# Where the small groups of experts stand in a streamed mixture of experts, and the order of its last products

## The chip, the cores and the metric

One core of a Trainium2 chip. The time is the device time of one execution in microseconds (us), as the median of several runs. TensorE (PE) multiplies, ScalarE (ACT) and VectorE (DVE) take results out of PSUM, GpSimd (POOL) does elementwise work in SBUF, and SyncE (SP) issues nearly all DMA transfers from HBM.

## The reference, cut to what matters

One decoder block for 256 tokens of width 1024, all in float32: attention and a gated recurrence, a normalisation, and then a mixture of 64 experts of which each token uses 8, beside a shared expert and an embedding term; a last normalisation ends it. The part that matters here:

```
idx, g = route(h, w_router[l], router_bias[l])            # 8 of 64 experts a token
for each expert e:                                        # xb: the tokens that chose e
    a = silu(xb @ w_gate[e]) * (xb @ w_up[e])             # 1024 -> 256
    out = (a @ w_down[e]) * g_b[:, None]                  # 256 -> 1024
    acc = acc.at[tok_b].add(out)
x = layer_norm(DEEPNORM_ALPHA * x1 + acc + shared + ple, ln2_w[l], ln2_b[l])
```

Each expert has 3 MB of weights, so 192 MB go through the core whatever the routing.

## The kernel before, in words

The first 380 us or so compute attention, the recurrence and the first normalisation. From then on the kernel streams expert weights. An expert's weights come as three transfers of 1 MB: n=0 and n=1 hold the gate and up columns of the first and the second half of the 1024 inputs, n=2 the down weights, whose columns 0 to 1023 give the first 512 outputs (f=0) and columns 1024 to 2047 the last 512 (f=1). Each transfer lands in one of 20 slots of 1 MB (`slot()`, rings of 9, 6, 2, 2 and 1), handed out in turn; a transfer into a slot waits until the products that read the slot's last content are done. SP issues all of them (`load`, line 81), each behind the one before; at most eight are under way.

The experts are sorted by how many tokens chose them (`rank`), all but the first eight. Those with most tokens are worked off two at a time, 64 token places each; the 24 with fewest are worked off four at a time, 32 places each (`SMALL` = 24). A unit (`units`) is two calls of `experts`: four experts where a call takes two, eight where a call takes four. There are ten units of pairs and three of groups of four. `SMALL_AT` gives the places at which the three are put among the others.

In a call of `experts`, `gate_up` (line 833) runs over the eight input blocks kt, and in each over the experts e, one product a step: the stationary operand is the expert's 64 or 32 token columns, the moving one 512 weight columns, and expert e writes its own 64 or 32 partitions of the PSUM tile `g`. Then `h` (line 800 and 802), two transposes of `h`, a copy `hT` (line 928), and the down products into a tile `g` for f=0 and one for f=1, over ft (the two halves of the 256 hidden values) and in each over the experts. Each `g` is scaled and split into `yh` (ACT, line 939) and `yl` (DVE, line 940), and four products with `sT` put it back to the tokens in `acc`; the two for f=1 are left to the next call (`rest`). In between, the calls gather the tokens of the next unit (tile `t` from `sel` and `xh`, `xl`). TensorE's order in this stage is that of the code (`PE_FIXED`).

In the last unit both calls load their weights as halves of 512 KB (`parts = 2`): of n=0 first half of every expert, then second half of every expert, and so on. Two slots more are taken there, for the rows of the last normalisation's weights and for their spread form `lw` (line 972); the first call spreads them by `norm_weights`, one row at each of its four steps. After the last call come `bn_stats`, `last_norm` and the stores.

Of the kernel before, what the change touches and what calls it, by code (L numbers as in the profile page):

```python
# [30 lines left out]
PE_FIXED = True  # L31
SB = 3
WARM, YB, TB, W2 = 8, 2, 2, 3
FIXED, SMALL, SMALL_AT = 8, 24, (2, 6, 9)
ROUTER_SPLIT = 4
WARM2 = 9
GS_POOL = (0, 2)
# [19 lines left out]
def tile_block(ctx: ExitStack, tc: tile.TileContext, a, out: bass.AP):  # L57
# [14 lines left out]
    def slot(dt=F32):  # L72

        pl, n = free[0]
        free.rotate(-1)
        return pl.tile([128, 2048], dt, name="raw", tag="raw", bufs=n)
# [3 lines left out]
    def load(dst, src, ordered=False):  # L80
        ins = nc.sync.dma_start(dst, src)
        loads.append(ins)
        if ordered:
            tc.keep_in_program_order(ins)
# [13 lines left out]
    def pinned(ins):  # L98
        if fixed["pe"]:
            tc.keep_in_program_order(ins)  # L100

    def mm(o, l, r, start=True, stop=True):
        pinned(pe.matmul(o, l, r, start=start, stop=stop))  # L103

    def transpose(o, t):
        pinned(pe.transpose(o, t, ident))  # L106
# [44 lines left out]
    for n in range(4):  # L151
        sl, c = slice(2 * n, 2 * n + 2), slice(512 * n, 512 * n + 512)
# [262 lines left out]
    def gates():  # L415
        gp = transposed(next_win())
        t = ptg.tile([128, 2, S], F32, name="tg", bufs=4)
        act.activation(t, gp, AF.Tanh, scale=0.5)
        return t
# [131 lines left out]
    def bank(tag, shape=(128, 512)):  # L551

        return pm2.tile(list(shape), F32, name=tag, tag=tag, bufs=2)
# [205 lines left out]
    def one_hot(pl, pos_of, n, by=pool, w=SLOTS):  # L759

        s = pl.tile([128, 2, w * n], F32R, name="sel1", bufs=2)
        for i in range(2):
            for e in range(n):
                by.tensor_scalar(s[:, i, w * e:w * e + w], iota[:, 0:w], pos_of(i)[:, e:e + 1], None, op0=OP.is_equal)  # L764
        return s
# [28 lines left out]
    def unit(u):  # L794
        r0, n = units[u]
        s, xe = one_hot(px2, lambda i: posm[:, i, r0:r0 + 2 * n], 2 * n, pool if u else dve, 128 // n), []
        return s, xe, gather(new_xe, bank, s, 4, xe)

    def swiglu(h, ps):
        act.activation(h, ps[:, 0:256], AF.Sigmoid)  # L800
        for n in range(2):
            dve.tensor_mul(h, h, ps[:, 256 * n:256 * n + 256])  # L802
# [18 lines left out]
    def expert_weights(r0, ne, last=False):  # L821

        w = [[] for _ in range(ne)]
        at = [expert_at(r0 + e) if r0 >= FIXED else None for e in range(ne)]
        for n in range(3):
            for e in range(ne):
                w[e].append(slot())
            parts = 2 if last else 1
            for part in range(parts):
                c = slice(2048 * part // parts, 2048 * (part + 1) // parts)  # L830
                for e in range(ne):
                    if at[e] is None:
                        load(w[e][n][:, c], a["exp"][3 * (r0 + e) + n][:, c])
                    else:
                        load(w[e][n][:, None, c], a["exp"][bass.ds(at[e] + n, 1)].rearrange("o p f -> p o f")[:, :, c], True)
        return w

    def gate_up(gu, kts, xe, off, w):
        n = 128 // len(w)
        for kt in kts:  # L840
            for e in range(len(w)):
                mm(gu[n * e:n * e + n], xe[kt // 2][:, kt % 2, off + n * e:off + n * e + n],
                   w[e][kt // 4][:, 512 * (kt % 4):512 * (kt % 4) + 512], start=kt == 0, stop=kt == KT - 1)
# [8 lines left out]
    s, xe, steps = unit(0)  # L852
# [17 lines left out]
    hT = bank("t", (128, 2, S))  # L870
# [7 lines left out]
    gu0 = bank("g")  # L878
# [16 lines left out]
    p3 = t2.enter_context(tc.tile_pool(name="p3", bufs=1, reuse_waits="tile"))  # L895


    def experts(pl, bk, xe, off, s, gates, w, add, before=(), steps=(iter(()),) * 4, begun=None):


        ne, sl = len(w), 128 // len(w)
        if begun is None:
            begun = bk("g")
            gate_up(begun, range(4), xe, off, w)
        next(steps[0], None)
        gu = begun
        gate_up(gu, range(4, KT), xe, off, w)
        h = pl.tile([128, 256], F32, name="h", bufs=1)
        swiglu(h, gu)
        next(steps[1], None)  # L910
        tr = bk("t", (128, 256 + 2 * ne))
        for i in range(2):
            transpose(tr[:, 128 * i:128 * i + 128], s[:, i, off:off + 128].bitcast(F32))
        for i in range(2):
            mm(tr[:, 256:256 + 2 * ne], s[:, i, off:off + 128], gates(i).rearrange("p e n -> p (e n)"), start=i == 0, stop=i == 1)
        sT = pl.tile([128, S], F32R, name="sT", bufs=TB)
        act.activation(sT, tr[:, 0:256], CP)
        gsl = pl.tile([128, 1], F32, name="gsl", bufs=3)
        for e in range(ne):
            dve.reduce_sum(gsl[sl * e:sl * e + sl], tr[sl * e:sl * e + sl, 256 + 2 * e:258 + 2 * e],  # L920
                           axis=mybir.AxisListType.X)
        for _ in before:
            pass
        tr = bk("t", (128, 2, 128))
        for ft in range(2):
            transpose(tr[:, ft], h[:, 128 * ft:128 * ft + 128])
        hT = pl.tile([128, 2, 128], F32, name="hT", bufs=1)
        dve.tensor_copy(hT, tr)
        next(steps[2], None)
        parts = []  # L930
        for f in range(2):
            y = bk("g")
            for ft in range(2):
                for e in range(ne):
                    mm(y[sl * e:sl * e + sl], hT[:, ft, sl * e:sl * e + sl],
                       w[e][2][:, 1024 * f + 512 * ft:1024 * f + 512 * ft + 512], start=ft == 0, stop=ft == 1)
            yh = pl.tile([128, 512], F32R, name="yh", bufs=YB)
            yl = pl.tile([128, 512], F32R, name="yl", bufs=YB)
            act.activation(yh, y, CP, scale=gsl)  # L939
            dve.scalar_tensor_tensor(yl, y, gsl, yh.bitcast(F32), op0=OP.mult, op1=OP.subtract)  # L940
            parts.append((yh, yl))

        def scatter(f):
            for i in range(2):
                add(i, f, sT[:, 128 * i:128 * i + 128], parts[f])
                yield

        next(steps[3], None)
        for _ in scatter(0):
            pass  # L950
        return scatter(1)

    stats = px.tile([128, 2, 2, 6], F32, name="stats")
    def norm_weights(rows, lw):

        for r in range(4):
            ps = bank("t")
            mm(ps, ident[:4, r:r + 1].to_broadcast([4, 128]), rows)
            act.activation(lw[:, r // 2, 512 * (r % 2):512 * (r % 2) + 512], ps, CP)
            yield  # L960
# [3 lines left out]
    for q, (r0, ne) in enumerate(units):  # L964
        if q + 1 < len(units):
            first = steps
            nxt, xnxt, steps = unit(q + 1)
            fill = ((none, steps, steps, none),) * 2
            if q == 0:
                fill = ((list(first) for _ in (0,)), steps, steps, none), fill[1]  # L970
        else:
            rows, lw = slot()[:4, :512], slot().rearrange("p (n d) -> p n d", n=2)
            for n, v in enumerate(("ln2w", "ln2b")):
                load(rows[2 * n:2 * n + 2], a[v].rearrange("(r f) -> r f", r=2), True)
            fill = (norm_weights(rows, lw),) * 4, (none,) * 4
        for pr in range(2):
            r = r0 + ne * pr
            last = q + 1 == len(units) and pr == 1
            w = expert_weights(r, ne, q + 1 == len(units)) if r else w0
            def add(i, f, l, halves, last=last):  # L980
                for n, r in enumerate(halves):
                    mm(acc[i][f], l, r, start=False, stop=last and n == 1)
                if last:
                    dve.bn_stats(stats[:, i, f], acc[i][f])

            rest = experts(p2, bank, xe, 128 * pr, s, lambda i: gates2[:, i, r:r + ne], w, add, rest, fill[pr],
                           None if r else gu0)
        s, xe = nxt, xnxt
    for _ in rest:
        pass  # L990
# [40 lines left out]
    with tc.If(nr > 1):  # L1031
# [7 lines left out]
        with tc.For_i(1, nr, 1):  # L1039
            dve.tensor_scalar(posm, posm, -float(SLOTS), None, op0=OP.add)  # L1040
            dve.memset(pair_no, 0.0)
            with tc.For_i(0, NE, 2) as c0:
                with tc.tile_pool(name="po", bufs=1) as po, \
# [4 lines left out]
                    w = []  # L1048
                    for e in range(2):
# [3 lines left out]
                        for n in range(3):  # L1053
                            t = slot()
# [16 lines left out]
                    s = one_hot(po, lambda i: pp[:, i], 2)  # L1071
                    xe = []
# [9 lines left out]
                    for _ in experts(po, obank, xe, 0, s, lambda i: gp2[:, i], w, add):  # L1082
                        pass
# [109 lines left out]
```

## Time and profile before

| | |
|---|---|
| median of 3 runs | 910.8 us (909.67 to 911.46) |
| the profiled execution's own time | 909.14 us |
| its span, first to last instruction | 907.4 us |
| mean granted TensorE clock | 0.985 of full |
| TensorE matmul busy | 856.1 us, 94% |
| expert transfers | 180 of 1 MB, 24 of 512 KB |

A busy TensorE is not one at its peak: products of different experts that run side by side count once in the busy time, however many they are. In the slices of the page (22.7 us each) the DMA engines are full from the twenty-first slice to the thirty-eighth; that is the stage of the experts. A float32 product appears in the trace as two MATMUL pieces, so `x32` in a row is 16 products. The chain of waits names for each stretch what was awaited last; the timeline gives single instructions.

### The profile page before, as it was taken

The page shows a single profiled execution, that of the slowest core. Times are in us where ns is not written, and L with a number is a line of the kernel's source. Part 1 is how long each engine was busy: PE and PEld are TensorE (multiplying, and loading weights), DVE is VectorE, ACT ScalarE, POOL GpSimd, SP SyncE. Part 2 cuts the span into 40 slices and gives each one's busy share as a digit, 9 for nine tenths or more (in the row PEclk, how much of TensorE's full clock was granted, in tenths as well). Part 3 has the DMA queues.
Part 4 walks back from the last instruction along what each step waited for, and adds up shares of the span by engine and source line. Part 5 has one row for each costly group of instructions (what it writes and reads, how often), then busy time and mean ns, then how long its engine had stood idle before and what let it go on. Part 6 is the DMA issues. An engine that isn't in the chain of part 4 may idle for free.

```text
span 907.4 us, 13967 instructions
## 1 busy us (share of the span) xinstructions
PE 856.1 (94%) x5200; PEld 567.4 (63%) x5200; DVE 380.8 (42%) x807; ACT 327.3 (36%) x652; POOL 171.9 (19%) x219
## 2 busy tenths in 40 slices
PE   9999999999999999799999999999689988799992
PEld 7899997878789999678545454544235433245431
DVE  5555555695966656887112222221112211112215
ACT  6444454567675555545212122121011211112221
POOL 0015463743400000542021011011010110101001
PEclk9999999999999999899999999999999998999997
DMA  8953433443334988344799999999999999999971
GB/s 335 420 221 122 140 103 130 149 140 129 128 129 163 388 299 303 117 182 186 297 391 407 415 421 421 420 421 420 420 421 420 420 421 421 421 420 421 410 300 48
DMA packets 42048, 270.84 MB, mean 298 GB/s; under 512 B 5061, under 2 KB 5189, under 8 KB 12281
## 3 DMA queue, kind: packets, MB, share of 16 engines
q1 hardware_dynamic: 41624, 269.20, 74.6%
q8 instruction: 42, 0.69, 0.3%
q10 hardware_dynamic: 288, 0.52, 0.2%
q14 instruction: 30, 0.24, 0.1%
q0 software_dynamic: 64, 0.20, 0.1%
HBM read 268.85 MB, written 1.05 MB: 297 GB/s over the span
## 4 chain that ended last, share of the span: by engine, by line
PE 76%; DMA 16%; DVE 5%; issue 1%; ACT 1%; SPq 0%; DVEq 0%
PE pj L103 26%; PE g L103 25%; DMA raw<-in_exp_dram 15%; PE t L103 6%; PE acc L103 6%; PE ah L103 4%; PE mix L472 2%; PE sc L103 2%; PE yp L103 1%; PE ap L381 1%; PE t L106 1%; PE pt L260 1%; DVE hr L365 1%; PE op L103 1%; DMA raw<-in_win_dram 0%
## 5 line engine op out<-in xcount | busy, mean ns | idle before, releaser
L103 PE MATMUL g<-raw,xe 128*64 128x512 f32 (+1 forms) x1024 | 203.9, 606 | 19.9 <-DMA raw<-in_exp_dram 19.9
L117 ACT ACTIVATE wh<-raw 128x512 fp32r<-128x512 f32 x213 | 132.3, 630 | 121.1 <-PE pj L103 86.5
L118 DVE TENSOR_TENSOR wl<-raw,wh 128x512 fp32r<-128x512 f32 x184 | 129.5, 715 | 90.7 <-ACT wh L117 69.8
L103 PEld LDWEIGHTS g<-raw,xe 128*64 128x64 f32 (+1 forms) x1024 | 59.7, 128 | 148.8 <-issue 109.0
L103 PE MATMUL pj<-xhi,wh 128*128 128x256 f32 x448 | 128.9, 288 | 0.2 <-DVE hq L366 0.2
L103 PE MATMUL pj<-xlo,wh 128*128 128x256 f32 x448 | 128.3, 286 | 0.0
L103 PE MATMUL pj<-xhi,wl 128*128 128x256 f32 x448 | 128.1, 286 | 0.0
L764 POOL TENSOR_SCALAR sel<-cst,posm 128x64 fp32r<-128x64 f32 (+1 forms) x120 | 48.0, 428 | 371.0 <-PE t L103 363.7
L802 DVE TENSOR_TENSOR h<-h,g 128x256 f32<-128x256 f32 x52 | 21.9, 421 | 228.6 <-ACT h L800 227.7
L103 PE MATMUL g<-raw,hT 128*64 128x512 f32 (+1 forms) x512 | 98.3, 598 | 4.3 <-DMA raw<-in_exp_dram 3.8
L800 ACT ACTIVATE h<-g 128x256 f32<-128x256 f32 x26 | 10.0, 383 | 222.5 <-PE g L103 222.5
L940 DVE SCALAR_TENSOR_TENSOR yl<-g,gsl,yh 128x512 fp32r<-128x512 f32 x52 | 39.0, 751 | 118.2 <-ACT yh L939 118.2
L103 PEld LDWEIGHTS pj<-xhi,wh 128*128 128x128 f32 x448 | 85.5, 191 | 3.5 <-issue 1.9
L103 PEld LDWEIGHTS pj<-xhi,wl 128*128 128x128 f32 x448 | 85.5, 191 | 3.1 <-issue 2.7
L103 PEld LDWEIGHTS pj<-xlo,wh 128*128 128x128 f32 x448 | 85.5, 191 | 2.7 <-issue 2.4
L118 POOL TENSOR_TENSOR wl<-raw,wh 128x512 fp32r<-128x512 f32 x29 | 38.4, 1333 | 156.8 <-ACT wh L117 140.4
L103 PEld LDWEIGHTS g<-raw,hT 128*64 128x64 f32 (+1 forms) x512 | 27.9, 126 | 55.9 <-issue 43.0
L939 ACT ACTIVATE yh<-g,gsl 128x512 fp32r<-128x512 f32 x52 | 35.7, 687 | 71.9 <-PE g L103 71.9
L103 PE MATMUL t<-sel,xh 128*128 128x256 f32 x208 | 56.1, 304 | 1.3 <-DVE gsl L920 1.3
L778 ACT ACTIVATE xe<-t 128x512 f32<-128x512 f32 x52 | 31.0, 597 | 68.9 <-PE t L103 68.9
L103 PEld LDWEIGHTS t<-sel,xh 128*128 128x128 f32 x208 | 39.2, 188 | 23.8 <-issue 22.7
L103 PE MATMUL t<-sel,xl 128*128 128x256 f32 x208 | 51.6, 281 | 0.0
(287 smaller groups left out, 1309.0 us busy)
## 6 DMA issues: line engine op xcount, KB each, us to landing
raw<-in_exp_dram SPq DMA_DIRECT2D x180, 1024.0 KB, 19.8
raw<-in_win_dram SPq DMA_DIRECT2D x40, 1024.0 KB, 6.4
raw<-in_exp_dram SPq DMA_DIRECT2D x24, 512.0 KB, 10.1
raw<-in_wab_dram SPq DMA_DIRECT2D x8, 768.0 KB, 5.5
raw<-in_wo_dram SPq DMA_DIRECT2D x4, 1024.0 KB, 8.0
raw<-in_pleg_dram SPq DMA_DIRECT2D x4, 1024.0 KB, 9.9
raw<-in_win_dram SPq DMA_DIRECT2D x8, 256.0 KB, 5.9
raw<-in_shgu_dram SPq DMA_DIRECT2D x2, 1024.0 KB
```

The lines of the kernel that those rows point to most:

```text
L103: pinned(pe.matmul(o, l, r, start=start, stop=stop))
L106: pinned(pe.transpose(o, t, ident))
L117: act.activation(hi, src, CP)
L118: (lo_engine or dve).tensor_sub(lo, src, hi.bitcast(F32))
L260: pe.transpose(pt[:, b], pr[:, 128 * b:128 * b + 128], ident)
L472: ins = pe.matmul(mix[i][f], l[:, ts], r[f], start=j == n == 0, stop=j == 7 and n == 2)
L764: by.tensor_scalar(s[:, i, w * e:w * e + w], iota[:, 0:w], pos_of(i)[:, e:e + 1], None, op0=OP.is_equal)
L778: act.activation(xe[k2], ps, CP)
L800: act.activation(h, ps[:, 0:256], AF.Sigmoid)
L802: dve.tensor_mul(h, h, ps[:, 256 * n:256 * n + 256])
L939: act.activation(yh, y, CP, scale=gsl)
L940: dve.scalar_tensor_tensor(yl, y, gsl, yh.bitcast(F32), op0=OP.mult, op1=OP.subtract)
```

## The change

`SMALL_AT` goes from (2, 6, 9) to (2, 7, 12): the first unit of groups of four stays where it is, the second comes after eight calls of pairs instead of six, and the third comes last of all, after eight more. So the last unit, whose transfers are halves, now has eight experts and 48 halves instead of four experts and 24. And in the very last call the products of f=1 go expert by expert, both ft of one expert before the next expert.

```
-FIXED, SMALL, SMALL_AT = 8, 24, (2, 6, 9)
+FIXED, SMALL, SMALL_AT = 8, 24, (2, 7, 12)
...
-            for ft in range(2):
-                for e in range(ne):
-                    mm(y[sl * e:sl * e + sl], hT[:, ft, sl * e:sl * e + sl],
-                       w[e][2][:, 1024 * f + 512 * ft:1024 * f + 512 * ft + 512], start=ft == 0, stop=ft == 1)
+            turns = [(ft, e) for ft in range(2) for e in range(ne)]
+            for ft, e in sorted(turns, key=lambda t: t[1]) if final and f else turns:
+                mm(y[sl * e:sl * e + sl], hT[:, ft, sl * e:sl * e + sl],
+                   w[e][2][:, 1024 * f + 512 * ft:1024 * f + 512 * ft + 512], start=ft == 0, stop=ft == 1)
...
             rest = experts(p2, bank, xe, 128 * pr, s, lambda i: gates2[:, i, r:r + ne], w, add, rest, fill[pr],
-                           None if r else gu0)
+                           None if r else gu0, last)
```

On TensorE, the gate and up products of the last call and what stands behind them, `-` before and `+` now:

```order
 L103 MATMUL acc<-yl,sT 128x512
-L103 MATMUL g<-raw,xe 64x512 x16
-L106 MATMUL t<-cst,sel_7909 128x128 x2
-L103 MATMUL t<-gates_4369,sel_7909 128x4 x2
+L103 MATMUL g<-raw,xe 32x512 x32
+L106 MATMUL t<-cst,sel_7785 128x128 x2
+L103 MATMUL t<-gates_4369,sel_7785 128x8 x2
 L103 MATMUL acc<-yh,sT 128x512
 L103 MATMUL acc<-yl,sT 128x512
```

The last call has 32 products of 32 columns where it had 16 of 64; the transposes and the products into `acc` around them are as many as before.

On TensorE, the down products of the last call now; each `raw` is one expert's down weights, `g_8348` is f=0 and `g_8361` is f=1 (before, both halves alternated between two tiles `raw`):

```order
L103 MATMUL g_8348<-raw_8278,hT_8346 32x512
L103 MATMUL g_8348<-raw_8279,hT_8346 32x512
L103 MATMUL g_8348<-raw_8280,hT_8346 32x512
L103 MATMUL g_8348<-raw_8281,hT_8346 32x512
L103 MATMUL g_8348<-raw_8278,hT_8346 32x512
L103 MATMUL g_8348<-raw_8279,hT_8346 32x512
L103 MATMUL g_8348<-raw_8280,hT_8346 32x512
L103 MATMUL g_8348<-raw_8281,hT_8346 32x512
L103 MATMUL g_8361<-raw_8278,hT_8346 32x512 x2
L103 MATMUL g_8361<-raw_8279,hT_8346 32x512 x2
L103 MATMUL g_8361<-raw_8280,hT_8346 32x512 x2
L103 MATMUL g_8361<-raw_8281,hT_8346 32x512 x2
```

In f=0 the four experts alternate; in f=1 both products of one expert follow each other.

On SP, where the transfers turn from whole ones to halves, now; `raw_8034` holds the rows of the normalisation, and four experts' tiles take turns behind it (before, two did, one unit later in the stream):

```order
L81 DMA raw_8034<-in_ln2w_dram 2x512
L81 DMA raw_8034<-in_ln2b_dram 2x512
L819 TENSOR_LOAD cst_105
L819 ISA x2
L819 TENSOR_LOAD cst_105
L819 ISA x2
L819 TENSOR_LOAD cst_105
L819 ISA x2
L819 TENSOR_LOAD cst_105
L819 ISA x2
L81 ISA
L81 DMA raw_8078<-in_exp_dram 128x1024
```

Four experts' places are read (`TENSOR_LOAD`) ahead of the first half where two were before.

## Rows read from the trace of the kernel before

**Rows 1.** The page: the span, TensorE's busy time, the rate in 40 slices.
```profile
span 907.4 us, 13967 instructions
...
PE 856.1 (94%) x5200; PEld 567.4 (63%) x5200; DVE 380.8 (42%) x807; ACT 327.3 (36%) x652; POOL 171.9 (19%) x219
...
GB/s 335 420 221 122 140 103 130 149 140 129 128 129 163 388 299 303 117 182 186 297 391 407 415 421 421 420 421 420 420 421 420 420 421 421 421 420 421 410 300 48
```

**Rows 2.** Busy time by stretch: engines' busy us (instructions), granted clock, DMA share, GB/s.
```profile
517.00:817.00 300.00, 275.47 (x1512) 121.76 (x1506) 51.16 (x123) 51.62 (x96) 30.54 (x80) 0.99 1.01 421
740.30:760.20 19.90, 16.41 (x88) 6.09 (x92) 1.89 (x7) 1.51 (x4) 0.00 (x0) 0.83 1.01 420
851.10:876.00 24.90, 24.90 (x109) 10.36 (x107) 5.65 (x13) 7.27 (x13) 0.00 (x0) 1.00 1.03 408
878.80:881.40 2.60, 2.60 (x14) 0.86 (x12) 0.00 (x0) 0.00 (x0) 0.00 (x0) 1.00 0.19 72
881.40:884.00 2.60, 2.60 (x15) 1.12 (x12) 0.18 (x1) 0.50 (x2) 0.00 (x0) 1.00 0.00 0
```

**Rows 3.** The chain of waits in order of time: start, us, what.
```profile
516.74 7.00 PE g L103 x64
...
532.53 7.02 PE g L103 x32
...
780.15 19.79 DMA raw<-in_exp_dram
799.98 3.65 PE g L103 x14
...
827.57 7.02 PE g L103 x32
...
843.05 7.02 PE g L103 x32
...
889.81 0.68 PE acc L103 x2
...
901.86 0.68 DVE o L1021
```

**Rows 4.** SP's last transfer of weights, in the timeline.
```profile
871.19 0.33 SPq L81 DMA_DIRECT2D raw<-in_exp_dram  x1
```

**Rows 5.** The page: issues of expert transfers, KB each, us to landing.
```profile
raw<-in_exp_dram SPq DMA_DIRECT2D x180, 1024.0 KB, 19.8
...
raw<-in_exp_dram SPq DMA_DIRECT2D x24, 512.0 KB, 10.1
```

**Rows 6.** The last call's gate and up and down products in TensorE's timeline.
```profile
876.27 7.09 PE L103 MATMUL g<-raw,xe 128*64 128x512 f32 x32
...
886.15 3.65 PE L103 MATMUL g<-raw,hT 128*64 128x512 f32 x16 [0.52 <-DVE hT L928]
```

**Rows 7.** The last call's two results taken out of PSUM, in ACT's timeline.
```profile
888.19 0.69 ACT L939 ACTIVATE yh<-g,gsl 128x512 fp32r<-128x512 f32 x1 [3.92 <-PE g L103]
889.92 0.69 ACT L939 ACTIVATE yh<-g,gsl 128x512 fp32r<-128x512 f32 x1 [1.04 <-PE g L103]
```

**Rows 8.** TensorE's timeline in a call of four that waits for transfers.
```profile
647.83 1.05 PE L103 MATMUL g<-raw,xe 128*32 128x512 f32 x2 [1.44 <-DMA raw<-in_exp_dram]
650.31 3.63 PE L103 MATMUL g<-raw,xe 128*32 128x512 f32 x28 [1.44 <-DMA raw<-in_exp_dram]
...
660.29 1.92 PE L103 MATMUL g<-raw,xe 128*32 128x512 f32 x16 [1.45 <-DMA raw<-in_exp_dram]
```

**Rows 9.** SP's waits from 517 to 850 us: total us, times, longest.
```profile
SPq L81 <- DMA raw<-in_exp_dram: 234.1, 129, 2.9
SPq L81 <- PE g L103: 3.8, 14, 0.4
```

**Rows 10.** TensorE's timeline in the later of the two units of four that wait.
```profile
745.17 1.04 PE L103 MATMUL g<-raw,xe 128*32 128x512 f32 x2 [1.32 <-DMA raw<-in_exp_dram]
747.65 1.91 PE L103 MATMUL g<-raw,xe 128*32 128x512 f32 x2 [1.44 <-DMA raw<-in_exp_dram]
```

More of the change, by code (lines that the diff above doesn't have):

```diff
@@ L895, in tile_block, with experts @@
     p3 = t2.enter_context(tc.tile_pool(name="p3", bufs=1, reuse_waits="tile"))
-    def experts(pl, bk, xe, off, s, gates, w, add, before=(), steps=(iter(()),) * 4, begun=None):
+    def experts(pl, bk, xe, off, s, gates, w, add, before=(), steps=(iter(()),) * 4, begun=None, final=False):
         ne, sl = len(w), 128 // len(w)
```

## The prediction, made before the changed kernel ran

> **What bounds the kernel now.** The page first: from the twenty-fourth slice on, the transfers run at 420 to 421 GB/s until the last three slices [rows 1], and the sums by stretch say the same of 517 to 817 us: 421 GB/s, DMA engines full [rows 2]. In that stage nothing but the rate of HBM sets the pace, although TensorE shows 94% busy. The reader is to see next, in the chain of waits, how TensorE stands to the stream. Gate and up products of successive calls of pairs begin at 827.57 and 843.05, so a call of two experts takes 15.48 us; its 6 MB (6.29 million bytes) arrive in 6.29/0.421 = 14.94 us. A call of four began at 516.74 and the next call at 532.53, 15.79 us, for 12 MB that need 29.9 us [rows 3]. So in each call of pairs TensorE falls 0.54 us further behind the stream, and in each call of four it gains up to 14.1 us.
>
> This decides the end. The last unit of four ends with the chain on a transfer (780.15, 19.79 us), and TensorE starts the six remaining calls of pairs at 799.98, right on the transfer [rows 3]. From there on it loses. The last weight transfer is issued at 871.19 [rows 4]; a half takes 10.1 us to land [rows 5], so it lands at about 881.3, and the stretch from 881.4 on shows 0 GB/s after 72 in the 2.6 us ahead of it [rows 2]. But TensorE begins the last call only at 876.27, ends its gate and up products at 883.36, starts the down products at 886.15 [rows 6], and the second result, f=1, is taken out of PSUM at 889.92 [rows 7]. That is 8.6 us after the last byte, all of it work that TensorE had left over. Behind it the chain goes on without a gap that anything else could fill: products into `acc` (889.81), statistics, last normalisation, the store after 901.86 [rows 3]. From 889.92 to the end of the span (907.4) [rows 1] it is 17.5 us, which the change doesn't touch: same four products, same order on DVE and ACT.
>
> **The change, part by part.**
>
> *The third unit of four comes last.* What goes: the 8.6 us between the last byte and the reading of f=1 lose TensorE's backlog. Call the landing of the last transfer T. In the last call, eight halves (n=2) follow the last of n=1, and four follow the last first half of n=2. At the 408 GB/s that halves had [rows 2], eight halves (4.19 million bytes) take 10.3 us, four 5.1. So the last gate and up weights land at T-10.3. Behind the last of four experts' transfers, eight products took 1.92 us [rows 8] (two steps, the four experts side by side), so gate and up end at T-8.4; from there to the down products it took 883.36 to 886.15, 2.8 us [rows 6], so these could start at T-5.6. Their first half has its weights at T-5.1. From the start of the down products (886.15) to the reading of f=0 (888.19) it took 2.04 us [rows 6, 7], two steps of products; so f=0 is out at T-3.1, while f=1's transfers still come. After T only the last expert's two products remain, again two steps: f=1 is read at T+2.0. The 8.6 us become 2.0: -6.6 us.
>
> *The last unit's transfers are halves*, and it now has 24 more, 12.58 million bytes: at 408 GB/s 30.8 us against 29.9 at 421 [rows 2], +0.9 us on T. From below it costs nothing (a stream kept full); from above twice that, since the 408 is a mean over bins of uneven pace. I take +1.0, so T = 882.3.
>
> *The second unit of four comes two calls of pairs later.* TensorE falls 2 x 0.54 = 1.1 us further behind ahead of it, and 8 x 0.54 = 4.3 us ahead of the third. That would cost only if a slot of the ring came free too late for SP. From 517 to 850 us, over a run of six calls that started behind the stream, SP waited 234.1 us for earlier transfers and 3.8 for TensorE, 0.4 at most [rows 9]. So the ring has room, and I take 0; if the room were used up, the price is at most the 1.1 us, once, since the unit of four behind it gains 14.1 a call. The four reads of expert places ahead of a call, instead of two, sit on SP between two issues; eight transfers (some 10.1 us of halves) are under way meanwhile [rows 5], so 0.
>
> *The slots.* The last unit now takes 24 slots and two for the normalisation's rows, out of 20: the last four go to slots of its first call, one of them the rows' own slot. The rows are read last in the fourth step of the first call, behind its down products, about T-31+2 (24 halves take 30.8 us); the transfer that needs the slot is issued 10.1 us and four halves (5.1) ahead of its landing, about T-15. 14 us of room: 0.
>
> *Expert by expert in f=1.* With the old order the last expert's first product would start at T, and the other three experts' second products beside it: after the last of four transfers, 28 pieces took 3.63 us [rows 8], four experts to a step. That is two steps after T, as now. I take 0. From above: the two products of one expert write the same partitions, so they can't run side by side; if each pair also held up the next expert's, the eight products, at 1.05 us for a single one [rows 8], would run 8.4 us from T-3.1 and end at T+5.3, 3.3 us later than taken. From below nothing is to be had, since two products of one expert need their two steps after T in any order.
>
> The Trainium skill says that tiles of the array work independently and that different tiles can load weights and multiply in parallel (TensorEngine Tiling (Array Packing), Key Properties). The trace agrees where experts alternate: 32 products of four experts took 7.00 us, 16 of two 7.02 [rows 3]. By that rule this order gives up the parallel run within an expert and gains nothing in return.
>
> **Sum.** -6.6 + 1.0 = -5.6 us: f=1 read at 884.3 instead of 889.92, span 901.8. The profiled execution took 909.14 us, 1.7 more than its span, and 1.7 less than the median of the runs, 910.8: so 903.5 for it, and 905.2 as a median.
>
> **The rivals.**
>
> A. *The order by expert is paid in full.* For it: nothing in the trace runs two products of one expert in succession while another waits. Against: pieces of four experts start within a step of one another, whatever the order in which their weights came [rows 8]. f=1 would be read at 882.3+5.3: 887.6, 2.3 us earlier than now: 908.5.
>
> B. *Slower: the clock falls in the last call.* TensorE now waits for transfers right to the end. In the later of the two units of four that wait, the granted clock was 0.83 on the mean of a call [rows 2], and a single product took 1.91 us instead of 1.04, at 1.2 instead of 2.4 GHz, after idle stretches of 1.3 and 1.4 us [rows 10]. If that meets the last call's down products, two steps take 3.8 us: f=0 is out at about T+0.1 (gate and up end later too), and f=1, run side by side, at T+3.9: 886.2, a median of 907.1. If the order by expert also runs one by one, 8 x 1.91 = 15.3 us: T+15.4 = 897.7, 7.8 us later than now: 918.6. It decides from T+7.6 on, where f=1 comes later than 889.92. Against it: halves come every 1.3 us, so the pauses are shorter than in that unit, and of four calls that waited one fell.
>
> The Trainium skill tells of a kernel whose waits for transfers let TensorE's clock fall again before every new block (TensorE: Matmul & The Clock Gate, HAM oscillation — how this bites in real kernels). [...]
>
> C. *The stream itself stalls in the last unit*, on the rows' slot or on the four reads. From the room worked out above it needs 14 us of delay on the slot; the reads could leave the stream empty for two or three us: about 908, and no change from 6.6 us of stall on.
>
> **How the numbers follow.** Forecast 0.80; A 0.08; B without the one-by-one order 0.04 (907.1), with it 0.03 (slower); C 0.05, half of it within 0.2% or worse. The runs shown differ by about 0.2%, 1.8 us, which is about what a measurement can tell from no change. Faster by more: forecast, most of A, B's milder form, half of C: 0.89; within: 0.07; slower: 0.04. The range: best case with halves at no cost and a little luck in the stream, -7.6: 903.2; at the other end A, 908.5, takes in B's milder form and most of C.
>
> **What would show it.** Right: the chain of waits ends its transfers only some 20 us ahead of the last store; the last weight transfer lands near 882; the down products of the last call run as 16 pieces of f=0 and then in groups that each wait for a transfer; ACT reads f=1 about 2.0 us after the last landing and 17.5 us before the end. The stretch from 517 us still shows 421 GB/s. Wrong: a clock below 1 in the last 15 us ahead of `bn_stats`; pieces of f=1 that follow each other one by one well past the last landing; SP waiting for TensorE by microseconds in the last unit; or landings of halves spaced wider than 1.3 us.

## The result, and the profile after

| | before | changed |
|---|---|---|
| median | 910.49 us (7 runs, 909.52 to 911.46) | 905.79 us (7 runs, 904.38 to 907.15) |
| ratio | | 0.995, 95% interval 0.9939 to 0.996 |
| profiled execution: time, span | 909.14, 907.4 us | 905.9, 904.1 us |

The changed kernel is 4.7 us faster, 3.6 to 5.6 by the interval; 5.6 was forecast. A second measurement beside other kernels (`c0_changed_again`, below) gave 0.9948, 0.9935 to 0.9962.

The chain of waits of the changed kernel, the columns as in [rows 3]:

```profile
762.25 19.73 DMA raw<-in_exp_dram
...
782.09 19.76 DMA raw<-in_exp_dram
...
801.97 19.84 DMA raw<-in_exp_dram
...
863.97 10.22 DMA raw<-in_exp_dram
...
874.24 1.92 PE g L103 x10
...
878.56 7.73 PE g L103 x32
...
898.35 0.68 DVE o L1021
```

In [rows 3] the chain left the transfers at 799.98 and ran on TensorE from there to the last products. Now it stays on transfers until 874.24, 30 us ahead of the end; 20 us ahead of the last store was the sign that the prediction named. The chain books the last down products as one stretch of TensorE (878.56, 7.73 us). That TensorE waits for transfers inside it is seen in its weight loads, below.

SP's last transfer of weights, what TensorE's weight loads waited for, and ACT's two readings in the last call, which answer to [rows 4, 6, 7]:

```profile
874.21 0.33 SPq L81 DMA_DIRECT2D raw<-in_exp_dram  x1
```
```profile
881.87 0.14 PEld L103 LDWEIGHTS g<-raw,hT 128*32 128x32 f32 x2 [0.19 <-DMA raw<-in_exp_dram]
...
883.13 0.14 PEld L103 LDWEIGHTS g<-raw,hT 128*32 128x32 f32 x2 [0.27 <-DMA raw<-in_exp_dram]
...
884.38 0.14 PEld L103 LDWEIGHTS g<-raw,hT 128*32 128x32 f32 x2 [0.25 <-DMA raw<-in_exp_dram]
```
```profile
881.36 0.69 ACT L939 ACTIVATE yh<-g,gsl 128x512 fp32r<-128x512 f32 x1 [4.31 <-PE g L103]
886.38 0.69 ACT L939 ACTIVATE yh<-g,gsl 128x512 fp32r<-128x512 f32 x1 [4.33 <-PE g L103]
```

The last three experts' products for f=1 each wait for a transfer, 1.25 us apart; the last begins at 884.38, within 0.1 us of the issue at 874.21 plus the 10.1 us that a half takes to land. ACT reads f=1 2.0 us later; before it was 8.6 us after the last landing.

Busy time by stretch of the changed kernel, columns as in [rows 2]; the second stretch is the last unit's transfers, the third and fourth its two parts:

```profile
519.00:819.00 300.00, 291.27 (x1556) 134.52 (x1550) 56.40 (x132) 58.16 (x108) 34.03 (x88) 0.99 1.01 420
821.80:876.00 54.20, 50.63 (x238) 15.28 (x234) 6.47 (x16) 7.66 (x14) 0.00 (x0) 1.00 1.02 405
...
824.00:834.00 10.00, 10.00 (x62) 5.44 (x65) 3.08 (x7) 3.18 (x6) 0.00 (x0) 1.00 1.00 384
834.00:876.00 42.00, 38.43 (x170) 9.20 (x162) 3.39 (x9) 4.43 (x8) 0.00 (x0) 1.00 1.03 410
```

The stream keeps its pace (420 against 421 GB/s) up to the last unit; in the halves it is 405, with a slow stretch of 384 where whole transfers give way to halves. There a half comes every 1.37 us, wider than the 1.3 that the prediction named as a sign of being wrong; after it, every 1.28.

One difference between the two profiles has nothing to do with the change. The program is the same on TensorE up to about 620 us, yet TensorE's clock is lower around 405 us in the changed kernel's profile. The stretch 400 to 415 us before, and then in the changed kernel:

```profile
400.00:415.00 15.00, 13.24 (x68) 10.15 (x67) 11.33 (x40) 5.60 (x11) 5.96 (x9) 1.00 0.35 126
```
```profile
400.00:415.00 15.00, 13.25 (x61) 9.90 (x60) 9.81 (x33) 4.71 (x9) 4.45 (x6) 0.89 0.27 87
```

In the chain of waits there, the same groups of products took 1.58 and 1.58 us before:

```profile
404.83 1.58 PE acc L103 x6
...
406.62 1.58 PE acc L103 x6
```

and 1.78 and 2.78 us in the changed kernel:

```profile
404.83 1.78 PE acc L103 x6
...
406.92 2.78 PE acc L103 x6
```

That is 1.4 us that the profile shown of before did not have to pay. In both profiles TensorE had just stood idle for 1.75 us, waiting for VectorE until 403.88; in the changed kernel's, the granted clock was then 0.52 on the mean of 406 to 408 us, nearly all at the lower of its two levels (1.2 and 2.4 GHz), and in that of before 1.00. It shows in nine of the ten other profiles of this study too, of the old order and the new; only `e9_norm_rows_earlier` is without it. So spans of two profiles can't be set against each other here, unless both have the fall or both lack it. The text below goes by medians, and inside a profile by the distance from the last landing (last issue and 10.1 us, or the wait that names it) to the reading of f=1. The median half takes 10.2 us to land in e4, e9 and e10, so a tenth less could stand there.

### The profile page after: what moved, and what is told of

It reads as the page before. It is cut to its first block, busy times and chain, and to the rows that moved or that the text cites. A ratio compares the mean times of both kernels' runs of the same rounds, so it can differ in the third digit from the quotient of the medians.

```text
span 904.1 us, 14001 instructions
## 1 busy us (share of the span) xinstructions
PE 865.0 (96%) x5200; PEld 569.6 (63%) x5200; DVE 380.8 (42%) x807; ACT 327.6 (36%) x652; POOL 172.0 (19%) x219
## 3 DMA queue, kind: packets, MB, share of 16 engines
HBM read 268.85 MB, written 1.05 MB: 299 GB/s over the span
## 4 chain that ended last, share of the span: by engine, by line
PE 66%; DMA 26%; DVE 5%; issue 1%; ACT 1%; SPq 0%; DVEq 0%
PE pj L103 26%; DMA raw<-in_exp_dram 26%; PE g L103 18%; PE acc L103 5%; PE t L103 4%; PE ah L103 4%; PE mix L472 2%; PE sc L103 2%; PE yp L103 1%; PE ap L381 1%; PE pt L260 1%; DVE hr L365 1%; PE t L106 1%; PE op L103 1%; DMA raw<-in_win_dram 0%
## 5 line engine op out<-in xcount | busy, mean ns | idle before, releaser
L103 PE MATMUL g<-raw,xe 128*64 128x512 f32 (+1 forms) x1024 | 207.5, 606 | 10.1 <-DMA raw<-in_exp_dram 10.1
L103 PE MATMUL g<-raw,hT 128*64 128x512 f32 (+1 forms) x512 | 102.5, 598 | 2.2 <-DMA raw<-in_exp_dram 1.7
## 6 DMA issues: line engine op xcount, KB each, us to landing
raw<-in_exp_dram SPq DMA_DIRECT2D x48, 512.0 KB, 10.1
```

## The experiments

Kernels that share a median of before ran on one chip beside the same runs of it; the ratios are to those.

| | edit | median, before beside it | ratio, 95% interval | f=1 read after last landing |
|---|---|---|---|---|
| e1_place_only | the places alone | 906.3, 909.98 | 0.9956, 0.9944 to 0.9967 | 2.0 us |
| e2_order_only | the order alone | 910.29, 909.98 | 1.0, 0.9991 to 1.0009 | 8.9 |
| e4_third_one_unit_earlier | (2, 7, 11) | 906.81, 909.98 | 0.996, 0.9947 to 0.9973 | 4.8 |
| e8_less_gather_at_end | before, less gather | 908.19, 909.98 | 0.9975, 0.9965 to 0.9986 | 6.8 |
| c0_changed_again | none | 906.14, 910.58 | 0.9948, 0.9935 to 0.9962 | 2.0 |
| e6_halves_last_down | 8 halves, not 48 | 903.58, 910.58 | 0.9926, 0.9913 to 0.994 | 2.0 |
| e7_quarters_last_down | 16 quarters | 902.02, 910.58 | 0.9911, 0.9898 to 0.9925 | 1.2 |
| e9_norm_rows_earlier | before, rows earlier | 906.21, 910.58 | 0.9956, 0.9942 to 0.9969 | 5.6 |
| e3_third_only | (2, 6, 12) | 905.85, 910.48 | 0.9948, 0.9931 to 0.9965 | 2.0 |
| e10_both_parts_of_backlog | e8 and e9 | 904.59, 910.48 | 0.9931, 0.9918 to 0.9944 | 3.7 |

**The two parts of the change, each alone.**

```
e1:  for ft, e in turns:                      # places (2, 7, 12)
e2:  FIXED, SMALL, SMALL_AT = 8, 24, (2, 6, 9) # order as changed
```

> The units' places of the change, but the last products in the old order, the experts alternating within each ft. Theory (TensorE's backlog at the end is what the change removes, the order by expert is worth nothing): as the changed kernel, 905.8 us, f=1 read about 2.1 us after the last landing. Rival (the order by expert carries part of the gain, because a product waiting for the last expert holds up the second products of the others): f=1 read about 2.9 us after the last landing, 906.7 us. Rival the other way (the order by expert costs): 905.0 us or less.

> The old places, the last products of f=1 expert by expert; here both experts' weights have landed long before. Theory: products of one expert queue on their own columns while the other expert's start beside them, so f=1 is read as before or at most one step (0.43 us) later: 910.5 to 911.0 us. Rival (each expert's products hold up the next expert's): four steps of about 0.87 us in place of two, f=1 read 3.4 to 3.8 us after f=0 instead of 1.7: 912.2 us.

The places carry the gain: 3.7 us, with an interval that overlaps that of the whole change, and f=1 is read 2.0 us after the landing. TensorE's timeline at the end of e1:

```profile
882.49 1.05 PE L103 MATMUL g<-raw,hT 128*32 128x512 f32 x2 [0.20 <-DMA raw<-in_exp_dram]
883.75 1.90 PE L103 MATMUL g<-raw,hT 128*32 128x512 f32 x10 [0.21 <-DMA raw<-in_exp_dram]
```

and ACT's reading behind it:

```profile
885.75 0.69 ACT L939 ACTIVATE yh<-g,gsl 128x512 fp32r<-128x512 f32 x1 [4.34 <-PE g L103]
```

After the last landing five products remain here, in 1.90 us; in the changed kernel two remain, one behind the other on the same partitions, and ACT reads as late. There are fewer products after the landing, but the same number of steps: the order by expert gives nothing. Nor does it cost anything that e2 can tell, whose interval reaches 0.8 us either way. In e2 all weights have landed when f=1 begins, and ACT reads f=1 1.77 us after f=0 (1.73 before, [rows 7]):

```profile
890.43 0.69 ACT L939 ACTIVATE yh<-g,gsl 128x512 fp32r<-128x512 f32 x1 [3.92 <-PE g L103]
892.20 0.69 ACT L939 ACTIVATE yh<-g,gsl 128x512 fp32r<-128x512 f32 x1 [1.08 <-PE g L103]
```

**Is it the backlog, or the group of four itself?** e4 puts one unit of pairs behind the third unit of four; e8 keeps the old places and leaves out the gather's products with `xl` for the last two units, whose token values so lose their low parts.

```
e4:  FIXED, SMALL, SMALL_AT = 8, 24, (2, 7, 11)
e8:  return s, xe, gather(new_xe, bank, s, 4, xe, u < 11)   # False: no products with xl
```

> The third unit of four stands last but one; one unit of pairs, in halves, comes behind it. Theory (backlog): two calls of pairs cannot fall behind by more than about 1 us, so TensorE waits for the transfers to the end here too. 24 fewer halves bring the last landing 1.0 us earlier; a last call of two needs its gate and up, then four steps of down products after it, so f=1 is read about 3.4 us after the landing instead of 2.1: about 906 us, 0.3 more than the changed kernel. Rival (it is the group of four itself, with thin products at the end, that gains): a last call of two costs what it did, about 909 to 910 us.

> The kernel before, with the second half of the gather's products (those with xl) left out for the last two units: some 16 products fewer in each of the two units before the last, about 1.0 us of TensorE in each of four calls of pairs, none of it in the last unit. Theory (backlog): f=1 is read about 4.0 us earlier, 4.6 us instead of 8.6 after the last landing, which itself does not move: 906.5 us. Rival (the end hangs on something of the last call itself, not on the backlog): 910.5 us.

Both went the way of the backlog, and both by less than I had worked out: e4 has f=1 4.8 us after the landing (872.28 issued, 887.22 read), not 3.4; e8 gained 1.8 us, not 4.0, with 6.8 us (873.23, 890.09). The last transfer of e8, and its reading of f=1:

```profile
873.23 0.33 SPq L81 DMA_DIRECT2D raw<-in_exp_dram  x1
```
```profile
890.09 0.69 ACT L940 ACTIVATE yh<-g,gsl 128x512 fp32r<-128x512 f32 x1 [1.04 <-PE g L103]
```

The chain of waits of e8 says why:

```profile
813.73 7.35 PE g L103 x32
...
828.65 7.36 PE g L103 x32
...
843.57 7.56 PE g L103 x32
...
858.69 3.58 PE g L103 x16
862.28 1.05 PE t L103 x2
863.33 3.58 PE g L103 x16
866.91 1.05 PE t L103 x2
...
869.71 1.05 PE t L103 x2
870.76 3.58 PE g L103 x16
874.34 1.05 PE t L103 x2
...
876.53 3.58 PE g L103 x15
```

The calls of pairs now begin 14.92 us apart, the last 15.12, which is about the stream's own pace: the 0.54 us of four calls, 2.2 in all, are gone or nearly so, and no more was there to take. But the first call of the last unit holds four products `t` of 1.05 us, one for each row of the last normalisation's weights, and the next call's gate and up come at 876.5 only, 17.8 us behind 858.69. So the backlog has a second part, which the prediction missed. It explains e4 as well: there the chain runs on TensorE from 850.78 on, through the same four products, although TensorE had waited for transfers up to that point.

**The second part, and both together.** In e9 the rows are spread in the third unit of four; e10 adds e8's edit (again without the products with `xl`).

```
+            if q == NORM_AT:                         # 9: the third unit of four
+                rows, lw = slot()[:4, :512], slot().rearrange("p (n d) -> p n d", n=2)
+                ...
+                nw = norm_weights(rows, lw)
+                fill = ((nw, steps, steps, nw),) * 2
         else:
-            fill = (norm_weights(rows, lw),) * 4, (none,) * 4
+            fill = (none,) * 4, (none,) * 4
```

> The kernel before, old places and old order, but the rows of the last normalisation are spread in the third unit of four, whose calls wait for transfers, and no longer in the last unit. Behind it stands what e8_less_gather_at_end left over: the first call of the last unit took TensorE 17.8 us from one gate and up to the next, against 14.9 of its transfers, four products of about 1.05 us for the rows among it. Theory (the backlog has two parts, 0.54 us in each of four calls of pairs, and these products): the last unit's first call shrinks by about 4 us, f=1 is read about 4 us earlier, some 4.7 instead of 8.7 after the last landing: 4 us faster than before. Rival (the products of the rows are hidden anyway): as before.

> The kernel before, old places and old order, with both of the earlier edits: the gather's second half left out for the last two units (the xl products), and the rows of the normalisation spread in the third unit of four. Theory (the 8.6 us from the last landing to the reading of f=1 are 3.4 us that a last call of two always needs, 2.1 us of four calls of pairs and about 3.1 us of the rows' products): f=1 read 3.4 to 3.7 us after the last landing, 905 us or a little less. Rival (some other work holds the last call back as well): 4.5 us or more after it.

e9, which leaves nothing out, is 4.4 us faster than before, 2.8 to 5.3, without moving a unit. The kernel before took 17.8 us from the first gate and up products of the last unit to those of its last call:

```profile
858.53 3.58 PE g L103 x16
...
876.34 7.02 PE g L103 x32
```

In the chain of waits of e9 it is 14.5:

```profile
843.02 7.02 PE g L104 x32
...
858.50 7.02 PE g L104 x32
...
873.02 7.02 PE g L104 x32
```

Its last transfer, and its reading of f=1:

```profile
870.87 0.33 SPq L82 DMA_DIRECT2D raw<-in_exp_dram  x1
```
```profile
886.54 0.69 ACT L940 ACTIVATE yh<-g,gsl 128x512 fp32r<-128x512 f32 x1 [1.04 <-PE g L104]
```

That is 5.6 us after the landing, not the 4.7 that were expected: the rows' products were worth 3.0 us of the distance, not 4. The profiles of before and of e9 are the two without the fall of the clock, so their spans can be compared: 907.4 and 904.0, 3.4 us, inside the interval but less than the 4.4 of the medians.

e10's last transfer and its readings of f=0 and f=1:

```profile
872.58 0.33 SPq L82 DMA_DIRECT2D raw<-in_exp_dram  x1
```
```profile
884.69 0.69 ACT L941 ACTIVATE yh<-g,gsl 128x512 fp32r<-128x512 f32 x1 [3.86 <-PE g L104]
886.42 0.69 ACT L941 ACTIVATE yh<-g,gsl 128x512 fp32r<-128x512 f32 x1 [1.04 <-PE g L104]
```

882.7 to 886.42 are 3.7 us: the account closes. Of the 8.6 us before, 3.7 are left with both parts gone, 1.8 to 1.9 belong to the calls of pairs (8.6 less the 6.8 of e8, 5.6 of e9 less 3.7), and 3.0 to 3.1 to the rows' products (8.6 less 5.6, 6.8 less 3.7). That all of the 3.7 is what a last call of two needs is not shown: 3.4 were worked out for it, and the chain of e10 still runs on TensorE through its last call.

**The second unit of four.**

```
e3:  FIXED, SMALL, SMALL_AT = 8, 24, (2, 6, 12)
```

> The changed kernel with the second unit of four back at its old place: (2, 6, 12). Theory (only what stands last matters, the ring has room for ten calls of pairs in a row): as the changed kernel, about 906 us, 4.7 faster than before, f=1 read 2.1 us after the last landing. Rival (the second unit's place keeps TensorE close to the stream and is needed): ten calls of pairs behind the second unit let TensorE fall 5.4 us behind, and if the ring lacked room, SP would wait for TensorE and the last landing come a us or more later: 907 us or more.

As the changed kernel, 4.6 us faster than before (3.2 to 6.3). Ten calls of pairs in a row do no harm, so the second unit's place is worth nothing that these runs can tell.

**The price of halves, and a faster version.** The changed kernel again, and two that keep whole transfers but for the very last down weights; e7 alternates the experts as before.

```
e6:  w = expert_weights(r, ne, last) if r else w0          # halves in the last call only
     parts = 2 if last and n == 2 else 1
e7:  parts = 4 if last and n == 2 else 1                   # and: for ft, e in turns
```

> The changed kernel once more, unaltered, beside the next three, for a closer interval: 5.6 us by the prediction's sum, 4.7 measured so far. Should the sum be right and the first runs low by chance: 5 to 6 us faster than before; should something of about 1 us be missing in the sum: 4 to 5.

> The changed kernel with whole transfers in the last unit, except for the down weights of the very last call, which stay halves: 8 halves in place of 48. Theory (halves cost about 0.04 us each on the last landing, and the end follows the last landing by 2.1 us): the last landing comes 1.5 us earlier, f=1 is read 2.1 us after it: 904.3 us. Rival (the halves buy an earlier start of gate and up that is then missing): f=1 later than 2.1 us after the landing, no gain, 905.8 us.

> As e6_halves_last_down, but the very last call's down weights come in quarters of 256 KB, one for each ft of each half, and the experts alternate within ft as before. After the last landing one step of products remains instead of two: f=1 read about 1.2 us after it; 16 quarters may cost the stream some 0.3 us. Theory: 903.7 us. Rival (small transfers slow the stream more than a step is worth): 905 us or more.

The changed kernel repeats its 4.4 us in the medians (0.9948 is 4.7): the lower of the two expectations. e6 is 2.6 us faster than the changed kernel beside it in the medians and 2.0 by the ratios, whose intervals just touch, so the 1.5 expected are not ruled out. Its rate in the last unit is 418 GB/s where the changed kernel has 405, and at the unit's start (the second line) it has no slow stretch:

```profile
821.00:876.00 55.00, 46.62 (x243) 15.95 (x240) 7.00 (x18) 8.42 (x16) 0.00 (x0) 0.94 1.01 418
...
821.00:830.00 9.00, 9.00 (x51) 4.76 (x47) 2.33 (x6) 2.54 (x5) 0.00 (x0) 1.00 1.01 421
```

e7 has the lowest median, 902.02 us, 8.1 us below the kernel before by its ratio; its interval overlaps that of e6, so it is not shown to be faster than e6. The waits of its last weight loads, and the reading of f=1:

```profile
883.59 0.14 PEld L103 LDWEIGHTS g<-raw,hT 128*32 128x32 f32 x2 [0.34 <-DMA raw<-in_exp_dram]
884.22 0.14 PEld L103 LDWEIGHTS g<-raw,hT 128*32 128x32 f32 x2 [0.49 <-DMA raw<-in_exp_dram]
```
```profile
885.37 0.69 ACT L939 ACTIVATE yh<-g,gsl 128x512 fp32r<-128x512 f32 x1 [2.02 <-PE g L103]
```

One step of products is left after the last landing, and f=1 is read 1.2 us after it, as expected. But the landing itself is late in this profile: from 870 to 884 us, while the quarters arrive, the stream has 261 GB/s, and the last one lands at 884.2, against 881.0 in the profile of e6. The profile of e7 is of its slowest execution (905.01 us) and that of e6 of its fastest (901.99), so what the quarters cost the stream in most executions stays open; the 0.3 us allowed for it are not borne out by this one.

## Why the prediction was right, point by point

*What bounds the end* was right: the stream sets the pace, and after it came work that TensorE had left over. The 8.6 us became 2.0, as forecast, in the changed kernel, its repeat, e1 and e3. Where it came from was read only in part, and "all of it work that TensorE had left over" goes too far: 3.7 us stay in e10, with both parts of the leftover gone. The prediction named 0.54 us a call of pairs for it. Six calls at that are 3.2 us, and with the 3.7 that stay anyway 6.9, not 8.6: the account did not close, and was not drawn up. Only four calls lose (the last unit gathers nothing), and the rest is the rows' products in the last unit's first call; the move hides them as well, because a call of four waits for its transfers anyway. The size of the step came out right because it was taken from the distance in the trace, not from a count of calls.

*The halves* were the mis-sized term. 24 more were priced at 1.0 us. The last unit's 25.2 million bytes at 405 GB/s take 62.1 us; the same bytes before, half at 421 and half at 408, 60.7: 1.4 us. In the other three profiles of this order (400 GB/s in c0, 407 in e1, 404 in e3) it is 1.1 to 2.2. e6, which has 40 halves fewer, gains 2.0 to 2.6 us, or 1.2 to 1.5 for 24 in proportion. With 1.1 to 2.2 in place of 1.0 the sum is -4.4 to -5.5 us, which takes in the 4.7. Closer than that the runs can't tell.

*The second unit's place* at 0 and *the slots* at 0 were right: SP's waits in the changed kernel, from 519 to 875 us, show TensorE at 0.4 us at most, as in [rows 9]:

```profile
SPq L81 <- DMA raw<-in_exp_dram: 239.3, 154, 3.0
SPq L81 <- PE g L103: 3.2, 10, 0.4
```

*Expert by expert* at 0 was right, and for the reason given. Rival A falls: products of one expert queue for their own partitions and do not hold up the next expert's, by e2's 1.77 us, and by the changed kernel, where the pairs of products start 1.25 us apart although the last pair takes 1.9 us. The rule of the Trainium skill that tiles of the array work independently (TensorEngine Tiling (Array Packing), Key Properties) agrees with both.

*Rival B* did not come: the granted clock was 1.00 through the changed kernel's last unit, where single products came every 1.3 us with pauses of 0.25. With whole transfers it did come for a while, ahead of the down products. In e6 the clock is 0.57 on the mean of 868 to 872 us, and in e7 0.57 from 872 to 874 and 0.58 to 876, behind single products of about 1.05 us with pauses of 1.3 to 1.5; in e7 the 26 pieces there took 5.13 us, where 28 took 3.63 at full clock [rows 8]:

```profile
872.63 5.13 PE L103 MATMUL g<-raw,xe 128*32 128x512 f32 x26 [1.47 <-DMA raw<-in_exp_dram]
```

In both the clock is back at 1.00 from 876 us on, so a fall that meets the down products was not seen, and its price is not tested. The kernel of which the Trainium skill tells that its clock falls again before every new block (TensorE: Matmul & The Clock Gate, HAM oscillation — how this bites in real kernels) waits longer for each block than any call here does, so these runs do not test that. *Rival C* did not come as a stall of microseconds: in the changed kernel's last unit SP's waits show TensorE at 0.4 us at most. The slow stretch of 384 GB/s isn't from the four reads of expert places either, since e6 has them at the same place and runs at 421.

*The absolute time*, 905.2 for 905.8, is closer than it should be. In the profile the last landing came at 884.3 instead of 882.3, and the span was 904.1 instead of 901.8. Some 1.4 us of that are the fall of the clock, which the profile of before did not have, about half a microsecond the halves, and 0.2 the way from f=1 to the end (17.7 us, not 17.5). The 1.7 us between the profile of before and its median was treated as an offset between profile and runs, and added; that most other profiles have the fall suggests that part of it was the fall, though which of the unprofiled executions had it is not shown. That the two nearly cancel was luck.

*The chance of "faster"* is added up a little low: 0.80, most of 0.08, 0.04 and half of 0.05 are over 0.90, not 0.89.

## What to carry to other kernels

Where transfers set the pace, look at what the compute engine still has to do after the last byte, and put the work with the least computing per byte last. Count what the last stages add beside the repeated work: here four small products in the wrong call cost more (3 us) than four calls of falling behind (2 us), and moving them alone brought 4.4 us in the medians, 3.4 by the spans of two profiles, of the 4.7 that the whole change did. Cut transfers small only where the end waits for them: whole ones everywhere but for the very last weights gave the lowest medians, 902 to 904 us.

## What the runs showed of the hardware that was not expected

Halves of 512 KB, eight under way, ran at 410 GB/s once settled and at 384 in the first 10 us (371 to 395 in c0, e1 and e3), against 420 for transfers of 1 MB. What makes the switch slow was not tested. And TensorE's clock fell or did not fall at the same place of the same program from one execution to the next: 0.89 or 1.00 on the mean of 400 to 415 us, behind the same idle stretch of 1.75 us. That is 1.4 us of the chain, not far from the 1.8 us that e8 gained.
